# A hybrid encoder layer: the right-hand tile pools of SBUF moved down by 1,664 bytes, the left-hand pool one tile shorter

## The chip, the cores and the metric

The kernel runs on one core of one Trainium2 chip. The metric is the time on the device in microseconds (us) of one execution; the median of three runs is quoted. One further execution was profiled instruction by instruction, and all rows below come from it.

The engines are named as the profile names them: PE is TensorE's matmul, PEld its weight load, DVE is VectorE, ACT is ScalarE, POOL is GpSimd, SP is SyncE (which here only issues DMAs). A matmul has a **stationary** operand (128 columns, brought into the array by a LDWEIGHTS) and a **moving** operand (up to 512 columns, streamed through it). Both are read from SBUF, the on-chip memory with 128 partitions; a place in SBUF is a byte address within the partition.

## The reference

One layer with 512 positions of width 1024, all in float32:

```python
h = rmsnorm(x, norm_mix_g)
x_rnn, g_rnn, u, v, gate_a, gate_b = split(h @ w_in)        # 1280, 1280, 1024, 1024, 1024, 1024
ya = rg_lru(causal_conv(x_rnn), ...) * gelu(g_rnn)           # recurrent branch
ya = ya @ w_branch_a
yb = gelu(u) * (w_s_masked @ layernorm(gelu(v)) + b_s)       # spatial gating branch, 128-position blocks
yb = yb @ w_branch_b
x = x + (sigmoid(gate_a) * ya + sigmoid(gate_b) * yb) @ w_out
f = square(relu(rmsnorm(x, norm_ffn_g) @ w_up))
x = x + f @ w_down
out = rmsnorm(x, final_norm_g)
```

## The kernel before

**Arithmetic.** Every large product is made of three matmuls in a reduced float32 format: each operand is split into a rounded part (names ending in h, for instance `whi`, `xg3h`) and a remainder (`wlo`, `xg3l`), and `mm3` (L262, L263, L264) issues h by h, h by l and l by h into one PSUM tile. One such matmul has 128 stationary columns and 512 moving ones. ACT makes the rounded part (L129, L132), DVE the remainder (L130, L133).

**Stages, in the program's order.** L is a line of the kernel.

- `v` and `u` (L337, `tok_half`): 2 halves each of 8 times 12 matmuls, 384 in all. Here the *stationary* operand is a 128-column piece of the activations `xg` and the *moving* operand is the weight tile (`whi`, `wlo`).
- `x`, `g`, `ga`, `gb` (`col_tile`): 10, 10, 8 and 8 column tiles of 8 times 3 matmuls. Here the weight block (512 bytes wide) is stationary and `xg` is moving. Between them stand the spatial mixing (`mix`, 8 times 3 matmuls), its transposes (`ybT`), the recurrence's gates (`gate`, L520 and L521) and `bb` (moving operand `yb`).
- `ba` (moving `ya`) and `o` (moving `mg`): the same `col_tile`, 8 tiles of 30 and 8 of 24 matmuls.
- `up` (moving `x2`, 32 tiles of 24 matmuls), in turns with the down products `p` (L728: stationary factor pieces, moving weights), and at the end `w` (L757, the same roles as `p`).

**Order.** PE's order is fixed when the program is built: `ORDER` gives the sequence of the column tiles, `later(n, ...)` puts vector work n tiles behind, and a scheduler at build time merges the streams. On the chip each engine runs its own list in order and waits on semaphores. Weights come in units of 512 KB: SP issues the load (L181), ACT and DVE split it, and 24 matmuls use it up.

**Places in SBUF.** Pools of the left side are laid from low addresses up, pools with `side="right"` from the end (byte 229,344) down. In the built program the left pools hold the weight tiles (`wp`, bytes 22,848 to 67,904), then `tp` (52 tiles of 2,048 bytes with the tag `t2`, and two slightly longer `xrp` tiles; it holds `yb`, `ya`, `mg`, the mixing operands `ws`, `vn` and all temporaries; it ends at 178,544) and, after `tp` is closed, `mp` of the channel MLP (67,904 to 178,496). All their matmul operands start at byte 320 modulo 2,048, or a multiple of 512 bytes behind it. On the right stand `pad` (32 bytes, never read), then 24 tiles of `xp` (the sixteen `xg` tiles and eight `u`), and later in the same bytes 24 of `x2p` (`x2` and its two parts). These start at byte 180,160 plus multiples of 2,048, which is 1,984 modulo 2,048.

So a right-hand tile is the moving operand of x, g, ga, gb and up: 240 + 240 + 192 + 192 + 768 = 1,632 matmuls; it is the stationary operand of v and u, 384 matmuls. In the other 512-column stages both operands are left-hand tiles.

```python
x_stack, t_stack = ExitStack(), ExitStack()
xp = x_stack.enter_context(tc.tile_pool(name="xp", bufs=24, side="right", reuse_waits="tile"))
...
x2p = ctx.enter_context(tc.tile_pool(name="x2p", bufs=24, side="right", reuse_waits="tile"))
```

## Time and profile before

| what | value |
|---|---|
| median of 3 runs | 810.34 us (809.98 to 810.74) |
| the profiled execution, its own time | 810.42 us |
| its span, first to last instruction | 808.6 us |
| PE busy | 798.5 us, 99% of the span, 3,496 matmuls |
| DVE busy | 493.6 us, 61% |
| ACT busy | 452.4 us, 56% |
| POOL busy | 61.1 us, 8% |

The 1.8 us between the profiled execution's time and its span lie before the first and behind the last instruction. Busy shares are averages over stages that differ. Matmuls are pipelined, so a row's duration (390 ns or so) overlaps with that of the next; what one matmul costs the stream is the distance from its start to the next one's start.

### The profile page before, as it was taken

Reading aid. Unit: us, or ns where it says so; the run is one execution under the profiler, and the core shown is the slowest. Engines: PE = TensorE matmul, PEld = TensorE weight load, DVE = VectorE, ACT = ScalarE, POOL = GpSimd, SP = SyncE. Lnnn points to the kernel's source line nnn. Section 1 sums busy time; section 2 is a strip of 40 time slices with the busy share of each in tenths; the row PEclk is TensorE's granted clock in tenths of the full one; section 3 lists DMA queues with packets and bytes.
Section 4 is the critical chain, followed back from the end, with each engine's and each line's share of the span. In section 5 each row is a group of like instructions: output and inputs, shape, how many; then the busy total and the mean of one; then the engine's idle time right before and its main releaser. Section 6 shows DMA issues by size and latency. Waiting matters only on the chain.

```text
span 808.6 us, 9094 instructions
## 1 busy us (share of the span) xinstructions
PE 798.5 (99%) x3496; PEld 650.9 (80%) x3496; DVE 493.6 (61%) x646; ACT 452.4 (56%) x552; POOL 61.1 (8%) x67
## 2 busy tenths in 40 slices
PE   9999999999999999999999999999999999999995
PEld 7888888888888888888888888888888888888884
DVE  6767774866656677654545453866477546754543
ACT  7454447668789888782224354545455545554423
POOL 6000000000000000000002300000000000000000
PEclk9999999999999999999999999999999999999999
DMA  7532331213323332223325470456635664575002
GB/s 262 196 105 99 110 118 53 91 56 114 107 77 105 118 104 85 90 100 105 105 78 161 166 285 26 105 154 184 182 79 155 202 170 97 148 187 135 0 1 104
DMA packets 29563, 97.38 MB, mean 120 GB/s; under 512 B 3536, under 2 KB 3536, under 8 KB 29520
## 3 DMA queue, kind: packets, MB, share of 16 engines
q1 hardware_dynamic: 22608, 77.66, 28.4%
q0 software_dynamic: 3456, 12.58, 8.3%
q10 hardware_dynamic: 3456, 6.56, 2.6%
q8 instruction: 27, 0.44, 0.2%
q14 instruction: 16, 0.13, 0.1%
HBM read 82.11 MB, written 2.10 MB: 104 GB/s over the span
## 4 chain that ended last, share of the span: by engine, by line
PE 98%; DMA 0%; DVE 0%; ACT 0%; SPq 0%; issue 0%; ACTq 0%
PE p L728 14%; PE up L264 7%; PE up L262 7%; PE up L263 7%; PE v L337 6%; PE u L337 6%; PE w L757 5%; PE g L262 2%; PE g L264 2%; PE x L264 2%; PE x L262 2%; PE g L263 2%; PE x L263 2%; PE ba L263 2%; PE ba L264 2%; PE ba L262 2%
## 5 line engine op out<-in xcount | busy, mean ns | idle before, releaser
L129 ACT ACTIVATE whi<-wraw 128x1024 fp32r<-128x1024 f32 (+1 forms) x87 | 90.5, 1045 | 108.5 <-issue 43.6
L130 DVE TENSOR_TENSOR wlo<-wraw,whi 128x1024 fp32r<-128x1024 f32 (+1 forms) x87 | 107.0, 1232 | 35.6 <-ACT whi L129 35.5
L646 DVE SCALAR_TENSOR_TENSOR f<-up,r_b 128x512 f32<-128x512 f32 x32 | 22.0, 690 | 75.8 <-PE up L264 75.6
L537 DVE SCALAR_TENSOR_TENSOR w<-w,s 128x512 f32<-128x512 f32 x10 | 6.9, 692 | 59.6 <-ACT w L532 59.6
L221 ACT ACTIVATE whi<-wraw 128x1024 fp32r<-128x1024 f32 x24 | 25.2, 1051 | 26.7 <-PE up L263 26.7
L223 POOL DMA_DIRECT2D wlo<-wraw x24 | 20.8, 865 | 254.5 <-ACT wlo L222 213.8
L129 ACT ACTIVATE whi<-raw0b 128x1024 fp32r<-128x1024 f32 x14 | 14.9, 1062 | 29.5 <-PE up L263 22.3
L129 ACT ACTIVATE whi<-raw1b 128x1024 fp32r<-128x1024 f32 x14 | 14.9, 1062 | 25.1 <-PE up L263 15.5
L742 DVE TENSOR_TENSOR xk<-p,xk 128x512 f32<-128x512 f32 x42 | 27.3, 681 | 0.0
L222 ACT ACTIVATE wlo<-whi 128x1024 fp32r<-128x1024 f32 x24 | 25.4, 1057 | 0.5
L533 POOL TENSOR_TENSOR ig<-ig,xr 128x512 f32<-128x512 f32 x10 | 12.9, 1293 | 161.0 <-ACT ig L527 161.0
L129 ACT ACTIVATE whi<-raw2b 128x1024 fp32r<-128x1024 f32 x14 | 14.8, 1060 | 18.3 <-PE up L263 10.5
L757 PE MATMUL w<-whi,fw 128*128 128x512 f32 x64 | 24.9, 389 | 0.0
L757 PE MATMUL w<-wlo,fw 128*128 128x512 f32 x64 | 24.9, 389 | 0.0
L757 PE MATMUL w<-whi,lw 128*128 128x512 f32 x64 | 24.7, 389 | 0.0
L130 DVE TENSOR_TENSOR wlo<-raw2b,whi 128x1024 fp32r<-128x1024 f32 x14 | 17.1, 1223 | 12.4 <-ACT whi L129 12.3
L130 DVE TENSOR_TENSOR wlo<-raw1b,whi 128x1024 fp32r<-128x1024 f32 x14 | 17.1, 1224 | 9.9 <-ACT whi L129 9.6
L501 DVE SCALAR_TENSOR_TENSOR xr<-xrp,par_sb,xr 128x512 f32<-128x512 f32 x30 | 22.5, 749 | 0.7
L507 ACT ACTIVATE xra<-xr 64x512 fp32r<-64x512 f32 x10 | 6.3, 632 | 29.0 <-DVE xr L501 29.0
L728 PE MATMUL p<-whi,fh0p 128*128 128x512 f32 x56 | 21.9, 391 | 0.0
L728 PE MATMUL p<-wlo,fh0p 128*128 128x512 f32 x56 | 21.8, 390 | 0.0
L728 PE MATMUL p<-wlo,fh1p 128*128 128x512 f32 x56 | 21.8, 390 | 0.0
(848 smaller groups left out, 2420.6 us busy)
## 6 DMA issues: line engine op xcount, KB each, us to landing
wraw<-in_wall SPq DMA_DIRECT2D x109, 512.0 KB, 3.3
wlo<-wraw POOLq DMA_DIRECT2D x24, 512.0 KB, 4.5
raw0b<-in_wdn SPq DMA_DIRECT2D x8, 512.0 KB, 7.5
raw1b<-in_wdn SPq DMA_DIRECT2D x8, 512.0 KB, 4.2
raw2b<-in_wdn SPq DMA_DIRECT2D x8, 512.0 KB, 4.1
raw3b<-in_wdn SPq DMA_DIRECT2D x8, 512.0 KB, 3.9
xt<-in_xT SPq DMA_DIRECT2D x8, 256.0 KB, 5.6
xres<-in_xT ACTq DMA_DIRECT2D x8, 256.0 KB, 2.6
```

What stands on the lines that cost most here:

```text
L129: nc.scalar.activation(hi, src, AF.Copy)
L130: nc.vector.tensor_tensor(out=lo, in0=src, in1=hi.bitcast(F32), op=ALU.subtract)
L221: nc.scalar.activation(hi, src, AF.Copy)
L222: nc.scalar.activation(lo, hi.bitcast(F32), AF.Copy, scale=-1.0)
L262: nc.tensor.matmul(acc, lhs[0], rhs[0], start=start, stop=False)
L263: nc.tensor.matmul(acc, lhs[0], rhs[1], start=False, stop=False)
L264: nc.tensor.matmul(acc, lhs[1], rhs[0], start=False, stop=stop)
L337: nc.tensor.matmul(acc[b], xg[k][xi][:, b * P : (b + 1) * P], w[wi], start=k == 0 and i == 0, stop=k == KT - 1 and i == 2,)
L501: nc.vector.scalar_tensor_tensor(out=xr, in0=xrp[:, 1 + k : 1 + k + T], scalar=pc(C_CW + k * RT + j), in1=xr, op0=ALU.mult, op1=ALU.add)
L728: nc.tensor.matmul(bank[k][j], lhs[li], rhs[ri], start=first and kk == 0 and n == 0, stop=kk == HK - 1 and n == 2, skip_group_check=True,)
L742: nc.vector.tensor_tensor(out=x, in0=bank[k][j], in1=x, op=ALU.add)
L757: nc.tensor.matmul(bank[b], l, r, start=kh == 0 and half == 0 and k == 0 and n == 0, stop=end and k == 1 and n == 2)
```

## The change

`pad` grows from 32 to 1,696 bytes. The right-hand tiles then start at byte 178,496 plus multiples of 2,048: 320 modulo 2,048, as on the left. With 52 tiles `tp` would end at 178,544, 48 bytes too far, so it gets 51. The clearing of the first 8 columns of `pad` goes from DVE to POOL. PE issues the same matmuls in the same order, and so do the DMA queues their transfers.

```diff
     padp = ctx.enter_context(tc.tile_pool(name="padp", bufs=1, side="right"))
-    pad = padp.tile([P, 8], F32, name="pad")
-    nc.vector.memset(pad, 0.0)
+    pad = padp.tile([P, 424], F32, name="pad")
+    nc.gpsimd.memset(pad[:, 0:8], 0.0)
...
-    tp = t_stack.enter_context(tc.tile_pool(name="tp", bufs=52, reuse_waits="tile"))
+    tp = t_stack.enter_context(tc.tile_pool(name="tp", bufs=51, reuse_waits="tile"))
```

The program's start on POOL: the clearing of `pad` now stands ahead of the identity matrix `ident` and of the zeros in front of the convolution's first tile (`xrp`).

```order
 L884 MEMSET const-uint8-127 128x1
 L891 UNCONDITIONAL_BRANCH [waits barrier_Pool_Activation_PE_DVE_SP_gather]
+L94 MEMSET pad 128x8
 masks.py:197 MEMSET ident 128x128
 L494 MEMSET xrp_978 128x4
```

One MEMSET is added here; on DVE the same one is gone from ahead of the MEMSET of `ones`, and nothing else on either engine changes its place.

With one tile fewer, and with `mp` now beginning below a differently filled `tp`, tiles follow other tiles in the same bytes, and waits sit on other instructions. ACT, where the channel MLP begins (L809 loads the final gain `gfin`, L618 takes the root of the mean square `ms` that PE has summed, L632 copies transposed activations; a name ending in _49 is the semaphore of an engine or a DMA queue):

```order
 L610 ACTIVATE sqb_3640<-xres_3598 128x512
 L129 ACTIVATE whi_3710<-wraw_3609 128x1024 [waits DMAHW7_49,PE_49,Activation_49]
-L809 DMA gfin<-in_ln 128x1024
+L809 DMA gfin<-in_ln 128x1024 [waits PE_49]
 L618 ACT_TABLE_LOAD
-L618 ACTIVATE r_b<-ms_3695,eps_t 128x512 [waits PE_49]
-L632 ACTIVATE xk_0_3707<-x2T_0_3702 128x512 [waits PE_49,Pool_49]
+L618 ACTIVATE r_b<-ms_3695,eps_t 128x512
+L632 ACTIVATE xk_0_3707<-x2T_0_3702 128x512 [waits PE_49]
 L129 ACTIVATE whi_3752<-wraw_3667 128x1024 [waits DMAHW1_49,PE_49,Activation_49]
```

No row changes its place; the wait for PE moves from the root (L618) up to the load of `gfin`, two rows earlier, because `gfin` now lies where the summed squares `ssq2` were.

## Rows read from the trace of the kernel before

**Rows 1.** The page: busy time, share, instructions; granted PE clock in 40 slices.

```profile
PE 798.5 (99%) x3496; PEld 650.9 (80%) x3496; DVE 493.6 (61%) x646; ACT 452.4 (56%) x552; POOL 61.1 (8%) x67
...
PEclk9999999999999999999999999999999999999999
```

**Rows 2.** Waits of PE, whole span: us in total, times, longest.

```profile
PE warm L120 <- DVE sp L421: 1.1, 1, 1.1
PE v L337 <- ACT whi L129: 0.6, 1, 0.6
```

**Rows 3.** Timeline of PE, 206 to 220 us: start, duration, instruction.

```profile
206.17 0.40 PE L262 MATMUL x<-xg2h,whi 128*128 128x512 f32 x1
206.41 0.39 PE L263 MATMUL x<-xg2l,whi 128*128 128x512 f32 x1
...
220.17 0.40 PE L262 MATMUL g<-xg6h,whi 128*128 128x512 f32 x1
```

**Rows 4.** Timeline of PE, 579 to 591 us: two up tiles.

```profile
579.42 0.40 PE L262 MATMUL up<-x20h,whi 128*128 128x512 f32 x1
...
590.62 0.39 PE L728 MATMUL p<-whi,fh1p 128*128 128x512 f32 x1
```

**Rows 5.** Timeline of PE, 415 to 453 us: the o stage.

```profile
415.06 0.39 PE L262 MATMUL o<-mg0h,whi 128*128 128x512 f32 x1
...
453.14 0.39 PE L262 MATMUL o<-mg0h,whi 128*128 128x512 f32 x1
```

**Rows 6.** The chain that ended last: start, us until the next piece, what.

```profile
27.87 25.09 PE v L337 x108
52.96 44.62 PE u L337 x192
...
507.83 5.47 PE p L728 x24
...
756.64 42.17 PE w L757 x186
```

**Rows 7.** Timeline of PE, 129 us: a mix of left-hand operands behind gb.

```profile
129.01 0.40 PE L262 MATMUL mix<-vn4h,ws1h 128*128 128x512 f32 x1
...
129.71 0.40 PE L520 MATMUL gate<-xra,lw0h 128*128 128x512 f32 x1
```

**Rows 8.** Weight loads by form: busy us, mean ns of one, idle.

```profile
L728 PEld LDWEIGHTS p<-whi,fh0p 128*128 128x128 f32 x56 | 10.5, 188 | 2.3
...
L337 PEld LDWEIGHTS v<-whi,xg0l 128*128 128x128 f32 x8 | 1.5, 188 | 0.3
```

**Rows 9.** Busy us in 97 to 356: PE, PEld, DVE, ACT, POOL; clock; DMA.

```profile
97.00:356.00 259.00, 259.00 (x1136) 210.03 (x1135) 169.83 (x241) 200.43 (x243) 13.76 (x18) 1.00 0.28 91
```

**Rows 10.** Timeline of DVE and PE in the first half of v.

```profile
20.53 2.32 DVE L130 TENSOR_TENSOR wlo<-wraw,whi 128x1024 fp32r<-128x1024 f32 x1
...
24.10 1.10 PE L337 MATMUL v<-wlo,xg6h 128*128 128x512 f32 x4
```

**Rows 11.** Timeline of DVE and ACT, 312 to 317 us.

```profile
312.15 1.22 DVE L544 TENSOR_TENSOR_SCAN h<-a,w 128x512 f32<-128x512 f32 x1
...
316.01 0.63 ACT L129 ACTIVATE ya7h<-gr 128x512 fp32r<-128x512 f32 x1 [0.16 <-DVE gr L552]
```

**Rows 12.** Timeline, 465 to 474 us: where the channel MLP begins.

```profile
465.57 1.02 PE L617 MATMUL ms<-ssq,ones 128*128 128x512 f32 x2
465.61 0.33 ACTq L809 DMA_DIRECT2D gfin<-in_ln  x1
...
466.67 1.28 ACT L618 ACT_TABLE_LOAD   x1
...
472.15 1.29 DVE L646 SCALAR_TENSOR_TENSOR f<-up,r_b 128x512 f32<-128x512 f32 x2
...
473.17 0.48 PE L262 MATMUL up<-x20h,whi 128*128 128x512 f32 x1
```

**Rows 13.** Timeline of PE: the first matmuls of v.

```profile
6.30 1.23 PE L337 MATMUL v<-whi,xg0h 128*128 128x512 f32 x4 [0.57 <-ACT whi L129]
```

## The prediction

> **What bounds the kernel now.** [...] Then the waits of PE: there are two in the whole span, 1.7 us together, both before 6.3 us [rows 2]. So nobody keeps PE waiting afterwards; the time is the number of matmuls times the distance from one start to the next, plus the start (6.3 us) and an end of 808.6 - 798.8 = 9.8 us behind the last w [rows 6]. What can make this kernel faster is either fewer matmuls, which the change doesn't bring, or a shorter step.

> So I measured the step by stage. In x and g, where a right-hand tile is the moving operand, 60 matmuls lie between the first and the last row of [rows 3]: 14.00 us / 60 = 233.3 ns. In up, the other stage of that kind, 48 matmuls take 590.62 - 579.42 = 11.20 us, again 233.3 ns [rows 4]. In o, which runs the same lines L262 to L264 with the same kind of weight block as stationary operand but a left-hand tile as moving one, 168 matmuls take 38.08 us: 226.7 ns [rows 5]. The last stage, w, has all operands on the left too: 42.17 us / 186 = 226.7 ns [rows 6]. In v and u, where the right-hand tile is the stationary operand, the chain has 25.09 us / 108 = 232.3 ns and 44.62 / 192 = 232.4 ns [rows 6]. The two paces thus go with the side of one operand, not with the line, the engine loads or the time in the program. And the sides differ in the place modulo 2 KB: 320 on the left, 1,984 on the right.

> **The change part by part.**

> *Moving tiles.* 1,632 matmuls go from 1,984 to 320. Nothing in the trace shows a right-hand tile at 320, so the new step has to be bounded. The best case is o's 226.7 ns; the trace has no stage that is quicker. The nearest worse row is the pace of a p tile directly behind other work, 5.47 us / 24 = 227.9 ns [rows 6]. If the place isn't what counts, the step stays at 233.3. I take 226.7, since o differs from x and g in that operand alone: 1,632 x 6.6 ns = 10.8 us less.

> *Stationary tiles.* 384 matmuls of v and u: from 232.35 to 226.7, 384 x 5.65 ns = 2.2 us less. This rests on a second assumption, that the place counts for the stationary operand too. v and u also differ in changing the PSUM tile at every matmul and keeping one moving tile for four; but w changes its PSUM tile at every third matmul and has 226.7.

> *A disturbance in this picture.* The mix stage has both operands on the left and still goes at the slow pace: three matmuls in 0.70 us, 233 ns each [rows 7]. They follow directly on gb's right-hand matmuls. I read it as a pace that outlasts the switch by some matmuls; then the first ones behind the opposite switch are quick, and both fall away. Taken as 0; if mix gains as well, 24 x 6.6 ns = 0.16 us more, and I leave 0.5 us either way for all such edges.

> *One tile fewer.* The order of all rows stays, so a cost would be a wait for a tile's last reader. With 51 tiles I followed for each tile who had the same bytes before. The closest pair of the pool's common tiles is `ya7h`, written by ACT from 316.01, behind a tile that the scan reads until 312.15 + 1.22 = 313.37 [rows 11]: 2.6 us in hand. Cost 0; a shorter PE step moves both alike, by 3%.

> *The wait of gfin.* ACT's queue now holds the load back until PE has finished `ms`, at 465.57 + 1.02 = 466.59. Before, it was issued at 465.61. Behind it in ACT's queue stand the table load (466.67) and the root; they now begin after the issue of 0.33 us, at about 466.95, so 0.3 us later. The reciprocal and the first f follow them. f at 472.15 (1.29 us for two, so the first ends near 472.8) frees the PSUM tile that the third up tile takes at 473.17 [rows 12]. Of the 0.33 us in hand, 0.3 go to the delay, and PE comes 18 matmuls x 6.6 ns = 0.1 us earlier, so PE waits some 0.1 us. Bounds 0 and 0.3; I take 0.2.

> *The clearing of pad.* DVE's queue loses one MEMSET ahead of `ones`, POOL's gains one. The first v matmul waits for ACT's first split of the weights [rows 13], not for `ones`, so 0.

> *Can the others keep up?* In 97 to 356 us ACT is the next busiest, 200.43 of 259 us [rows 9]; that stage shrinks by some 7 us, to a share of 80%. The tightest place is the first half of v, where DVE finishes a remainder at 20.53 + 2.32 = 22.85 and PE needs it at 24.10 [rows 10]. PE gets there 0.4 us earlier (some 75 matmuls x 5.65 ns), and 0.8 us remain. DMA moves the same bytes.

> Sum: 10.8 + 2.2 - 0.2 = 12.8 us. From the profiled execution's own 810.42 us that gives **797.6 us**. That execution is 0.08 us above the median of the three runs, which I neglect.

> [...]

> **The rivals.**

> *Moving only.* The stationary operand's place does nothing, and v's and u's pace comes from their own pattern of PSUM tiles and repeated moving tiles. Then the gain is 10.8 - 0.2: 799.8 us. For it: no left-hand stage has that pattern. Against it: w, as said.

> *The place is not the cause.* In this trace each right-hand tile is both at 1,984 and above byte 180,160; no row parts the two. If the upper end of SBUF is read more slowly, or these stages have some other cause, the change does nothing for PE, and the 0.2 us of gfin remain: 810.6 us. For it: that confounding. Against it: a weight load from the right takes as long as one from the left, 188 ns both [rows 8], so distance alone shows nothing there. [...]

> *Slower: equal places collide.* If a moving tile, the next stationary block and the tiles being written at the same time get in each other's way when all start at the same place, the right-hand stages lose instead. In x the starts are 0.24 us apart at the most [rows 3]; were every step to become such a long one, 1,632 x 6.7 ns = 10.9 us: 821 us. It decides as soon as the mean step of those stages rises by more than 1 ns (1.6 us). Against it: o and w, where all operands start at 320 modulo 512 already.

> **How the numbers follow.** The forecast has a chance of 0.76, moving only 0.08, no effect 0.11, slower 0.05. By its own bounds the forecast reaches from 796.9 (edges +0.5, gfin 0) to 800.5 (steps of 227.9 ns, 2,016 x 1.2 ns = 2.4 us less gain, and the edges against me). With moving only, and a little for what I haven't seen, I give **796.2 to 801.5 us**, which leaves out the no-effect case and the slower one, 16 in 100. 0.2%, or 1.6 us, is about what a measurement of this kernel can tell from no change. Both first cases are faster by more: 0.84; no effect is the same: 0.11; slower 0.05.

> **What the profile after would show.** If I am right, 60 matmuls of x and g take 13.6 us, 48 of up 10.9, u's 192 43.5, mix goes at 227 ns, and PE has at most one new wait, short, near 473 us. If only v and u stay at 232 ns, it is the moving operand alone. If x and up stay at 233, the place was not the cause. I would be wrong in another way if the steps shrink and PE begins to wait for `wlo` or `whi`: then feeding it becomes the bound, first in v or in x to gb, and the gain stops early.

## The result and the profile after

The changed kernel takes 798.38 us (median of 4 runs, 797.94 to 800.49) against 810.35 us for the kernel before on the same chip (4 runs): ratio 0.9857, 95% interval 0.9839 to 0.9876, or 12.0 us less. The profiled execution took 797.95 us, with a span of 796.2 us.

From the page of the changed kernel: span; busy time, share and instructions; granted PE clock in 40 slices.

```profile
span 796.2 us, 9092 instructions
...
PE 786.5 (99%) x3496; PEld 649.9 (82%) x3496; DVE 492.5 (62%) x645; ACT 452.0 (57%) x552; POOL 61.1 (8%) x68
...
PEclk9999999999999999999999999999999999999998
```

The same 3,496 matmuls occupy PE for 12.0 us less, at the granted clock of [rows 1] (a mean of 0.996 over the span, before 0.998; only the last slice, in which the matmuls end, shows less). So the step has become shorter, and the timeline of the changed kernel shows where (start, duration, instruction; the first two rows and those from 457 to 466 us are for the waits further down):

```profile
21.00 2.30 DVE L130 TENSOR_TENSOR wlo<-wraw,whi 128x1024 fp32r<-128x1024 f32 x1
...
23.35 0.77 PEld L337 LDWEIGHTS v<-wlo,xg6h 128*128 128x128 f32 x4 [0.30 <-DVE wlo L130]
...
202.06 0.39 PE L262 MATMUL x<-xg2h,whi 128*128 128x512 f32 x1
...
215.66 0.39 PE L262 MATMUL g<-xg6h,whi 128*128 128x512 f32 x1
...
457.83 1.02 PE L617 MATMUL ms<-ssq,ones 128*128 128x512 f32 x2
...
458.89 0.34 ACTq L809 DMA_DIRECT2D gfin<-in_ln  x1
...
459.25 1.28 ACT L618 ACT_TABLE_LOAD   x1 [0.35 <-PE ms L617]
...
464.74 1.29 DVE L646 SCALAR_TENSOR_TENSOR f<-up,r_b 128x512 f32<-128x512 f32 x2
...
465.48 0.50 PE L262 MATMUL up<-x20h,whi 128*128 128x512 f32 x1
...
569.97 0.39 PE L262 MATMUL up<-x20h,whi 128*128 128x512 f32 x1
...
580.85 0.39 PE L728 MATMUL p<-whi,fh1p 128*128 128x512 f32 x1
```

The 60 matmuls of [rows 3] (18 of x, 24 of gb, 18 of g) now take 215.66 - 202.06 = 13.60 us, 226.7 ns each (before 233.3). The 48 of [rows 4] take 10.88 us, again 226.7 ns. The chain of the changed kernel (start, us until the next piece, what) answers to [rows 6]:

```profile
5.57 19.89 PE v L337 x84
...
27.21 24.53 PE v L337 x108
51.74 43.52 PE u L337 x192
```

u has come from 232.4 to 226.7 ns. The second half of v has 227.1 ns with a few longer steps in it. The first half took 19.89 us, about as long as before:

```profile
6.30 19.82 PE v L337 x84
```

The reason is that PE now waits for DVE there: the remainder of the weights that [rows 10] shows begins at 21.00, ends at 23.30, and the load of `v<-wlo` starts at 23.35 behind an idle time of 0.30 us. It is one of three such waits. From the waits of the weight loads, whole span (us in total, times, longest; before, no load waited for `wlo`, `yb7h` or `xrb`):

```profile
PEld v L337 <- DVE wlo L130: 0.9, 3, 0.3
...
PEld bb L262 <- ACT yb7h L129: 0.3, 1, 0.3
PEld gate L520 <- DVE xrb L510: 0.2, 1, 0.2
```

A matmul was still running during part of these waits; by the starts of the matmuls themselves, the three waits in v cost PE 0.4 us and the one in bb 0.2.

Summed over the starts of all matmuls in both profiled executions, the 12.4 us between them come from the stages with a moving right-hand tile (9.9), u (1.1), v (0.5), p (0.3), mix (0.1) and an earlier first v matmul (0.7), less 0.3 us in several small places, bb and the transposes `x2T` with 0.1 each among them. The 0.7 us are luck and not the change: the first weights were under way for 3.22 us instead of 3.95, and over the profiled executions here that matmul starts anywhere from 5.6 to 6.3 us (by the chains of all kernels but the one at 1,792, whose chain doesn't hold it).

### The profile page after: what moved, and what is told of

It reads as the page before. It is cut to its first block, busy times and chain, and to the rows that moved or that the text cites. A ratio compares the mean times of both kernels' runs of the same rounds, so it can differ in the third digit from the quotient of the medians.

```text
span 796.2 us, 9092 instructions
## 1 busy us (share of the span) xinstructions
PE 786.5 (99%) x3496; PEld 649.9 (82%) x3496; DVE 492.5 (62%) x645; ACT 452.0 (57%) x552; POOL 61.1 (8%) x68
## 4 chain that ended last, share of the span: by engine, by line
PE 98%; DMA 0%; DVE 0%; ACT 0%; SPq 0%; issue 0%; ACTq 0%
PE p L728 14%; PE up L262 7%; PE up L264 7%; PE up L263 7%; PE v L337 6%; PE u L337 5%; PE w L757 5%; PE g L262 2%; PE x L262 2%; PE g L264 2%; PE x L264 2%; PE ba L263 2%; PE ba L264 2%; PE x L263 2%; PE g L263 2%; PE ba L262 2%
## 5 line engine op out<-in xcount | busy, mean ns | idle before, releaser
L728 PE MATMUL p<-whi,fl0p 128*128 128x512 f32 x56 | 21.8, 389 | 0.0
L728 PE MATMUL p<-whi,fh1p 128*128 128x512 f32 x56 | 21.8, 389 | 0.0
```

The lines of the kernel that those rows point to most:

```text
L728: nc.tensor.matmul(bank[k][j], lhs[li], rhs[ri], start=first and kk == 0 and n == 0, stop=kk == HK - 1 and n == 2, skip_group_check=True,)
```

## The experiments

Two theories stood against each other. By the first, a matmul's step depends on the **distance** between the places of its two operands, modulo some number of bytes. By the second, a tile is slow or quick by its **own place**: modulo 2 KB, or by the part of SBUF it lies in. Each run is compared with the kernel before on the same chip. Distances below are the start of the moving tile minus that of the stationary block. All blocks within a tile are multiples of 512 bytes apart, so one number holds for a whole stage.

**The tile alone.** The right-hand tiles stay where they were.

```diff
-    nc.vector.memset(pad, 0.0)
+    nc.gpsimd.memset(pad[:, 0:8], 0.0)
...
-    tp = t_stack.enter_context(tc.tile_pool(name="tp", bufs=52, reuse_waits="tile"))
+    tp = t_stack.enter_context(tc.tile_pool(name="tp", bufs=51, reuse_waits="tile"))
```

> The change without its move: one tile fewer in the left-hand pool and the clearing of pad on GpSimd, but the right-hand tiles stay at 1,984 modulo 2,048. If the place makes the gain, the steps of x, g and up stay at 233.3 ns and the time at about 810.4 to 810.6 us. If the gain came from the tile, the clearing or their new waits, the time is about 798 us.

Measured: 810.24 us against 810.20, ratio 1.0002 (0.9992 to 1.0011). Its chain has the pace of before in u, 44.62 us:

```profile
52.64 44.62 PE u L337 x192
```

So neither the tile, nor its new waits, nor the clearing of `pad` on POOL has a cost or a gain that can be measured (the interval reaches from 0.6 us less to 0.9 us more); the move makes all of the 12 us.

**Right-hand tiles at 1,856.** All 52 tiles and all waits are as before.

```diff
-    pad = padp.tile([P, 8], F32, name="pad")
-    nc.vector.memset(pad, 0.0)
+    pad = padp.tile([P, 40], F32, name="pad")
+    nc.vector.memset(pad[:, 0:8], 0.0)
```

> Before with pad 128 bytes longer and nothing else: right-hand tiles at 1,856 modulo 2,048, which is 320 modulo 512 but not modulo 2,048; all 52 left-hand tiles and all waits as before. If the place modulo 512 bytes (or a part of it) is what counts, the whole gain comes: 226.7 ns in x, g, up and u, about 798 us. If it is the place modulo 2,048, as the change has it, or modulo 1,024, there is no gain: 233.3 ns and 810.4 us.

Measured: 798.49 us, ratio 0.9854 (0.9839 to 0.9869). From its chain, and from its timeline at two up tiles, 48 matmuls in 10.88 us:

```profile
5.70 19.38 PE v L337 x84
...
51.36 43.52 PE u L337 x192
```

```profile
569.93 0.39 PE L262 MATMUL up<-x20h,whi 128*128 128x512 f32 x1
...
580.81 0.39 PE L728 MATMUL p<-whi,fh1p 128*128 128x512 f32 x1
```

The whole gain comes with 128 bytes: 226.7 ns in u and in up. Equality modulo 2,048 isn't needed here, 512 is enough. The first half of v took 19.38 us here, with one wait of 0.18 us for DVE left of the three: where DVE hardly holds PE up, v gains as u does (84 x 5.65 ns = 0.47 us; before 19.82).

**The left-hand tiles moved instead.** The right-hand tiles keep 1,984.

```diff
-    const = ctx.enter_context(tc.tile_pool(name="const", bufs=1))
+    const = ctx.enter_context(tc.tile_pool(name="const", bufs=1)); lpad = ctx.enter_context(tc.tile_pool(name="lpp", bufs=1)).tile([P, 32], F32, name="lpad"); nc.gpsimd.memset(lpad[:, 0:8], 0.0)
```

> Before with 128 bytes put ahead of the left-hand pools: left tiles at 448 modulo 2,048, right-hand tiles untouched at 1,984, which is 448 modulo 512 as well. If the two operands' places relative to each other count, the whole gain comes though no right-hand tile has moved: about 798 us. If a place is slow by itself (1,984 or 448 modulo 512), the right-hand stages stay at 233.3 ns, and bb, ba, o, p and w join them: 1,320 matmuls x 6.6 ns = 8.7 us more, about 819 us.

Measured: 798.21 us, ratio 0.9851 (0.9836 to 0.9865). From its chain:

```profile
51.52 43.52 PE u L337 x192
...
744.44 42.17 PE w L757 x186
```

u, whose stationary tiles haven't moved by a byte, has the short step, 226.7 ns, and w has kept it, 226.7 as well. The part of SBUF isn't the cause, and neither is the place 1,984 by itself.

**Only the weight tiles moved.** 128 bytes ahead of `wp` and 384 behind it, with 51 tiles in `tp`.

```diff
-    const = ctx.enter_context(tc.tile_pool(name="const", bufs=1))
+    const = ctx.enter_context(tc.tile_pool(name="const", bufs=1)); lpad = ctx.enter_context(tc.tile_pool(name="lpp", bufs=1)).tile([P, 32], F32, name="lpad"); nc.gpsimd.memset(lpad[:, 0:8], 0.0)
-    wp = ctx.enter_context(tc.tile_pool(name="wp", bufs=3))
+    wp = ctx.enter_context(tc.tile_pool(name="wp", bufs=3)); mpad = ctx.enter_context(tc.tile_pool(name="mpp", bufs=1)).tile([P, 96], F32, name="mpad"); nc.gpsimd.memset(mpad[:, 0:8], 0.0)
...
-    tp = t_stack.enter_context(tc.tile_pool(name="tp", bufs=52, reuse_waits="tile"))
+    tp = t_stack.enter_context(tc.tile_pool(name="tp", bufs=51, reuse_waits="tile"))
```

> Only the weight tiles move, by 128 bytes, to 448 modulo 512; the other left-hand tiles stay at 320 modulo 512 (832 modulo 2,048), the right-hand ones at 1,984; one left tile fewer for room. If the relative place counts, the paces change places: x, g, ga, gb, up, v, u go to 226.7 ns (12.4 us less, as measured for the change), while bb, ba, o, p, w go to about 233 ns (1,320 x 6.6 ns = 8.7 us more): about 806.6 us. If each tile's own place counts, nearly all matmuls touch a slow place and the time is about 819 us.

Measured: 806.91 us, ratio 0.9957 (0.9943 to 0.9972). The paces have changed places. From its chain, and from its timeline (four o tiles of 24 matmuls):

```profile
52.10 43.52 PE u L337 x192
...
514.95 5.59 PE p L728 x24
...
752.18 43.23 PE w L757 x186
```

```profile
427.54 0.40 PE L262 MATMUL o<-mg0h,whi 128*128 128x512 f32 x1
...
449.94 0.40 PE L262 MATMUL o<-mg0h,whi 128*128 128x512 f32 x1
```

o takes 22.40 us / 96 = 233.3 ns (before 226.7, [rows 5]) and w 43.23 / 186 = 232.4 (before 226.7), while u is at 226.7. The p tile of the chain has 5.59 us / 24 = 232.9 ns. The forecast of 806.6 us from the distance alone is met within about 0.3. By a tile's own place it would have been 819.

**How far apart.** Six runs move only the right-hand tiles, by 8 to 96 more columns of `pad`, as in the run at 1,856. First 64, 192, 256 and 384 bytes:

> Right-hand tiles 64 bytes lower than before: distance to the left-hand places 64 modulo 512 (before 128, changed kernel 0). If only equality modulo 512 counts, the step of x and up stays at 233.3 ns: 810.4 us. If the penalty grows with the distance, about 230 ns and 804 us. If equality modulo 64 were enough, 226.7 ns and 798 us, but then the kernel before (128 apart) would have had the short step as well, so this last is ruled out already.

> Right-hand tiles 192 bytes lower: distance 448 modulo 512, that is 64 on the other side. Only equality: 233.3 ns, 810.4 us. Penalty by distance: as at 64, about 230 ns and 804 us. If the sign counts (who is ahead), this one and the one at 64 differ.

> Right-hand tiles 256 bytes lower: distance 384, that is 128 on the other side. Only equality: 810.4 us. Sign counts: other than the kernel before. In the kernel with only the weights moved both signs of 128 gave 232 to 233 ns, so all theories expect about 233 ns and 810 us here, unless the side matters by itself.

> Right-hand tiles 384 bytes lower: distance 256 modulo 512, and equal modulo 256. If equality modulo 256 is enough, 226.7 ns and 798 us. If it has to be 512, 233.3 ns and 810.4 us; if the penalty grows with the distance, more than at 128: 240 ns, 821 us.

Then two places that are no multiple of 64 bytes away:

> Right-hand tiles 96 bytes lower than before: the moving tile starts 32 bytes behind the stationary block modulo 256 in x, g, up, and 32 ahead of it (224) in v and u. If the step follows moving minus stationary modulo 256 without a jump (0: 226.7, 64: 228.9, 128: 232 to 233, 192: 233.3 ns), x and up have about 228 ns; and u, at 224, lies between 226.7 and 233.3. If it takes only the values at multiples of 64 bytes, x has 226.7 or 228.9. Time about 801 to 803 us.

> Right-hand tiles 32 bytes lower: moving minus stationary is 96 modulo 256 in x, g, up, and 160 in v and u. Without a jump: x and up between 228.9 and 233.3, about 231 ns, u about 233 ns; time about 807 to 808 us. If only equality modulo 128 or the nearest multiple of 64 matters, x has 228.9 or 233.3.

| right-hand tiles at | distance mod 256 in x, g, up | step of up, ns | distance mod 256 in v, u | step of u, ns | median, us | ratio (95%) |
|---|---|---|---|---|---|---|
| 1,600 | 0 | 226.7 | 0 | 226.7 | 799.41 | 0.9864 (0.9836 to 0.9893) |
| 1,888 | 32 | 233.5 | 224 | 233.3 | 811.59 | 1.0015 (1.0004 to 1.0027) |
| 1,920 | 64 | 229.2 | 192 | 233.3 | 805.50 | 0.9941 (0.9918 to 0.9964) |
| 1,952 | 96 | 233.8 | 160 | 234.3 | 812.37 | 1.0027 (1.0016 to 1.0039) |
| 1,728 | 128 | 233.1 | 128 | 232.3 | 810.20 | 1.0000 (0.9989 to 1.0011) |
| 1,792 | 192 | 233.1 | 64 | 228.9 | 809.65 | 0.9991 (0.9980 to 1.0002) |

Each step of up is that of two tiles, 48 matmuls, from the timeline; each of u is its 192 matmuls in the chain. For all but 1,728 these are the rows, run by run. At 1,600:

```profile
570.73 0.39 PE L262 MATMUL up<-x20h,whi 128*128 128x512 f32 x1
...
581.61 0.39 PE L728 MATMUL p<-whi,fh1p 128*128 128x512 f32 x1
```

```profile
51.88 43.52 PE u L337 x192
```

At 1,888:

```profile
579.82 0.40 PE L262 MATMUL up<-x20h,whi 128*128 128x512 f32 x1
...
591.03 0.40 PE L728 MATMUL p<-whi,fh1p 128*128 128x512 f32 x1
```

```profile
52.55 44.80 PE u L337 x192
```

At 1,920:

```profile
576.21 0.40 PE L262 MATMUL up<-x20h,whi 128*128 128x512 f32 x1
...
587.21 0.40 PE L728 MATMUL p<-whi,fh1p 128*128 128x512 f32 x1
```

```profile
53.05 44.80 PE u L337 x192
```

At 1,952:

```profile
580.66 0.40 PE L262 MATMUL up<-x20h,whi 128*128 128x512 f32 x1
...
591.88 0.40 PE L728 MATMUL p<-whi,fh1p 128*128 128x512 f32 x1
```

```profile
52.84 44.98 PE u L337 x192
```

At 1,792:

```profile
578.36 0.39 PE L262 MATMUL up<-x20h,whi 128*128 128x512 f32 x1
...
589.55 0.39 PE L728 MATMUL p<-whi,fh1p 128*128 128x512 f32 x1
```

```profile
52.13 43.95 PE u L337 x192
```

Three things follow. Equality modulo 256 bytes is enough here: at 1,600 the short step is all there, 226.7 ns in up and in u. The order of the two counts: 64 bytes with the moving tile behind (at the higher place modulo 256: up at 1,920, u at 1,792) cost 2.2 to 2.5 ns, 64 bytes with it ahead (192 in the table) 6.4 to 6.6. And my expectation of a slope without a jump fell: 32 bytes cost as much as 128 (233.5 ns in up at 1,888, 233.1 at 1,728), the runs at 1,888 and 1,952 took 812 us where I had 801 to 803 and 807 to 808, and both are a little slower than the kernel before, by 0.15% and 0.27%.

**Both sides 32 bytes further.** This asks whether the 32 bytes cost as a distance, or because a tile no longer starts at a multiple of 64.

```diff
-    const = ctx.enter_context(tc.tile_pool(name="const", bufs=1))
+    const = ctx.enter_context(tc.tile_pool(name="const", bufs=1)); lpad = ctx.enter_context(tc.tile_pool(name="lpp", bufs=1)).tile([P, 8], F32, name="lpad"); nc.gpsimd.memset(lpad[:, 0:8], 0.0)
-    pad = padp.tile([P, 8], F32, name="pad")
-    nc.vector.memset(pad, 0.0)
+    pad = padp.tile([P, 416], F32, name="pad")
+    nc.vector.memset(pad[:, 0:8], 0.0)
...
-    tp = t_stack.enter_context(tc.tile_pool(name="tp", bufs=52, reuse_waits="tile"))
+    tp = t_stack.enter_context(tc.tile_pool(name="tp", bufs=51, reuse_waits="tile"))
```

> The changed kernel with everything, left and right, 32 bytes further: all tiles at 352 modulo 2,048. If only the distance of the two operands counts, the step stays at 226.7 ns everywhere and the time at about 798.3 us, and the 32 bytes that cost all in the run at 1,888 did so as a distance. If an operand must itself start at a multiple of 64 bytes, all stages go to about 233 ns: (2,016 + 1,320) matmuls x 6.6 ns = 22 us above the changed kernel, about 820 us.

Measured: 797.93 us, ratio 0.9849 (0.9833 to 0.9866). From its chain:

```profile
51.53 43.52 PE u L337 x192
...
743.95 42.17 PE w L757 x186
```

u and w have 226.7 ns with all tiles at 352: the 32 bytes that gave u 233.3 ns at 1,888 cost as a distance, and not as a place.

**Only the remainder of the weights moved.** `wlo` starts 128 bytes off, `whi` doesn't. To `mpad` and the 51 tiles of the run with moved weights comes a spacer between the two tags:

```diff
-        hi = wp.tile([P, UB * P], F32R, tag="whi", name=f"whi{n}", bufs=4)
+        hi = wp.tile([P, UB * P], F32R, tag="whi", name=f"whi{n}", bufs=4); n == 0 and nc.gpsimd.memset(wp.tile([P, 32], F32, tag="gap", name="gap", bufs=1)[:, 0:8], 0.0)
```

> Only the remainder tiles of the weights (wlo) move, by 128 bytes; whi stays at 320 modulo 512, the other left tiles at 320 modulo 512, the right-hand ones at 1,984. In o the three matmuls of a block then have equal, equal and unequal operands. If each matmul pays for its own pair, the mean step of o is 226.7 + 6.6 / 3 = 228.9 ns, and in x, where two of three are unequal, 231.1 ns. If one unequal weight load slows the matmuls around it, o has up to 233 ns. If a matmul pays for the load of the next weights that runs beside it, the mean in o is again 228.9 but the long step belongs to the second matmul of a block, not the third.

Measured: 816.24 us, ratio 1.0076 (1.0046 to 1.0105). In o the distance is 0 for the first two matmuls of a block (L262, L263) and not for the third (L264), whose weights are loaded while the second runs (in the kernel before, at 430.25 us, that load and the second matmul start together). Its groups by form in 424 to 452 us (busy us, mean ns of one, idle):

```profile
L262 PE MATMUL o<-mg4h,whi 128*128 128x512 f32 x5 | 1.9, 389 | 0.0
...
L263 PE MATMUL o<-mg4l,whi 128*128 128x512 f32 x5 | 2.0, 396 | 0.0
...
L264 PE MATMUL o<-mg4h,wlo 128*128 128x512 f32 x5 | 2.0, 397 | 0.0
```

389 ns is the duration of a matmul with the short step. In o the second and the third matmul of a block are slow: from start to start, over 63 of its 64 blocks, the three take 226.7, 232.7 and 234.0 ns. None of the three ways that I had written down gives this. The mean in o is 231.1 ns, where two of the ways had 228.9 and the third up to 233. By o alone, an unequal block would cost two matmuls, the one beside which it is loaded and the one that uses it. Other stages of the same run speak against that as a rule. From its chain:

```profile
52.76 44.59 PE u L337 x192
...
521.72 5.59 PE p L728 x24
```

In p only one matmul of three, the one that moves `wlo`, has unequal operands, and the step is 5.59 us / 24 = 232.9 ns, the same as in the run with all weights moved, where all three have; the three take some 236, 234 and 230 ns. In u the matmuls that move `wlo`, a third of them, now have equal operands (both at 448 modulo 512), and still all of u takes 44.59 us, about as long as before; 64 matmuls at 226.7 ns instead of 232.4 would bring 0.36 us, by my estimate, and 0.03 came. So the step of one matmul doesn't follow from its own pair. The short step came in the long stages whose pairs were all equal; which matmuls pay in a mixed stage, and for how long after an unequal pair, isn't shown.

## Why the prediction was right

**The step.** I took 226.7 ns for the moved stages from o, between bounds of 226.7 and 233.3, and x, g, gb and up have 226.7 (the 60 matmuls of [rows 3], which I gave to x and g, hold 24 of gb; as it has the same roles, no term changes). The reading that the pace goes with where the operands lie, and not with the line or the stage, held: moving only the weights turned o and u round in one run. What the trace of before couldn't part, the upper end of SBUF against the place modulo some number, the run with moved left-hand tiles decided. One thing I had only half right: I spoke of a tile's own place, 1,984 or 320, and in the runs the step went with the distance between the two operands (226.7 ns in u at distance 0, with the tiles at 320, 352 or 448 modulo 512). The change makes all places equal, so both readings gave the same sum; that this difference didn't show in the time was luck. All three rivals are out: no effect, because the steps shrank; moving only, because u shrank too; slower, because no stage with moved tiles has a longer step. The step itself differed in the runs by up to 7.6 ns with that distance (u has 226.7 ns at 0 and 234.3 at 160, in the run at 1,952).

**Moving tiles, 10.8 us.** 9.9 came. The step was right; the edges cost the other 0.9: before, these stages took 0.5 us more than 1,632 steps of 233.3 ns, and now they take 1.4 us more than 1,632 of 226.7. Part of this had nothing to gain, since the second right-hand matmul behind another stage often had a short step before (224 or 225 ns in 22 of 25 places in up). The rest are longer steps near such changes, which stay. I had put all edges at 0 with 0.5 us either way; with the 0.3 us that p and the 0.1 that mix gave, they come to 0.5 against me, the end of that allowance.

**Stationary tiles, 2.2 us.** u gave its 1.1. v gave 0.5 in the profiled execution, since in its first half DVE finished the remainders too late for PE. I had 0.8 us in hand there, with the 0.4 us of the shorter steps already taken off. I had read PE's need off the matmul at 24.10, but it is the weight load that waits, and before it began at 23.87:

```profile
23.87 0.89 PEld L337 LDWEIGHTS v<-wlo,xg6h 128*128 128x128 f32 x4
```

So only 0.6 us were in hand. The first v matmul came 0.7 us earlier, and DVE began that remainder 0.5 us later (21.00 instead of 20.53), which together is more than that. Both go back to when the two pieces of the first weights land: ACT splits them from 5.62 us on in one go before, and at 4.89 and 6.39 now. In the run at 1,856 one wait of 0.18 us was left and v gave 1.0. So the term was right in size, and the cover was thinner than the working had it.

**Mix.** The mixing matmuls came from 232 to 228 ns on average, as the carry-over would have it, and so did the first three matmuls of p behind up (from 231 or 232 to 227), which is p's 0.3 us. But the run with moved remainders shows in o a first matmul with the short step directly behind two slow ones. So why three of mix's matmuls were slow is left open.

**One tile fewer, the wait of gfin, pad.** I had 0, 0.2 and 0 us. The run with these alone gave a ratio of 1.0002. The wait is there as described: the load of `gfin` is issued at 458.89, right behind the sums that end at 458.85, ACT stands idle for 0.35 us ahead of the table load, and the third up tile starts at 465.48, just behind the first f (464.74 + 0.69). PE lost 0.02 us by it: the first step of that up tile is 338 ns, before 316. The transposes ahead of it, `x2T`, take 0.1 us more: 3.21 us against 3.08 before and at 1,856, with 52 tiles. So the one new wait that I had expected is hardly one. The new ones that came, in v, bb and gate, I had not counted, though I named v as the first place where feeding PE could become the bound.

**The time.** 797.6 was forecast, 798.38 measured. The profiled execution, at 797.95 us, is 0.4 above the forecast: the edges (0.9), v's first half (0.6) and bb (0.1), less p and mix (0.4), for which I had taken 0, and less the lucky start (0.7). Without that start the profiled execution would have been about 1 us above the forecast, so part of the closeness is luck. The other 0.4 us lie between it and the median of the four runs. One of the four, at 800.49 us, stands 2.5 us above the lowest, more than the kernel before spread in any of the five comparisons (at most 1.2); what made it so isn't known.

## What to carry to other kernels

## What the runs showed of the hardware

All of this was measured on matmuls with 128 stationary columns and 512 moving ones of 4-byte elements, at a mean granted clock of 0.996 to 0.998 of full speed. The mean step of a long row whose pairs all have the same distance (of the moving tile's start behind the stationary block's, modulo 256 bytes) was:

- at 0: 226.7 ns in up and u of the changed kernel and of the runs at 1,856 and 1,600, in u and w with the left-hand tiles moved or with all tiles at 352, and in o and w of the kernel before; 227.1 in the second half of v of the changed kernel and in two up tiles with moved weights (10.90 us / 48);
- at 64: 229.2 in up at 1,920, 228.9 in u at 1,792;
- at 128: 233.3 in x and up before and in o with moved weights, 233.1 in up at 1,728; 232.3 to 232.4 in v and u before, in u at 1,728 and in w with moved weights;
- at 192: 233.1 in up at 1,792, 233.3 in u at 1,920;
- at 32, 96, 160 and 224: 233.5 (up at 1,888), 233.8 (up at 1,952), 234.3 (u at 1,952) and 233.3 (u at 1,888).

The three places tried at distance 0, 320, 352 and 448 modulo 512, gave u the same 226.7 ns. Single steps don't repeat the mean: before, nearly all of the 48 of [rows 4] alternate between 229 ns and 237 to 238, whichever of the three lines they belong to. In a stage with equal and unequal pairs, matmuls with equal operands were slow too (with `wlo` moved, the second matmul of a block in o: 232.7 ns from start to start). What in the memory or the engine makes this wasn't shown.
